# A chunked RWKV-7 recurrence with its first product in one full-width matmul, under a list schedule of best-of-six passes

## The chip, the cores and the metric

The kernel runs on one core of a Trainium2 chip. The metric is device microseconds (us) of one execution, smaller is better. The engines are named as the profile names them: PE multiplies matrices (PEld loads its weights), DVE and ACT work on vectors, POOL does slower vector work, SP issues DMAs.

## The reference

One layer of a hybrid decoder trunk, sequence 4096, width 1024, float32. The input is normalised, projected by one matrix of 3728 columns, and read by two groups of heads: four heads of gated linear attention (GLA), and eight RWKV-7 heads of size 64. Their outputs are gated, concatenated, projected, added to the input and normalised. The part that this change is about is the RWKV-7 state update, one step per token:

```python
def step(S, inp):
    r_t, w_t, k_t, v_t, kk_t, a_t = inp
    sa = jnp.einsum('bhvk,bhk->bhv', S, -kk_t)
    S = (S * w_t[:, :, None, :]
         + sa[..., None] * (kk_t * a_t)[:, :, None, :]
         + v_t[..., None] * k_t[:, :, None, :])
    y = jnp.einsum('bhvk,bhk->bhv', S, r_t)
    return S, y
```

Every head has a 64x64 state. Each token decays it, corrects it along one direction (the delta rule), adds an outer product, and reads it with `r_t`.

## The kernel before, in words

**Tiling.** The sequence is cut into 8 blocks of 512 tokens (`TB`). Eight heads are handled as four pairs `p`, one head on partitions 0 to 63 (`lo`) and one on 64 to 127 (`hi`). A *unit* `u` is one pair in one block, so there are 32 units. Inside a unit the tokens are taken in `NC` = 8 chunks of 64 (`C`). All projections are float16 matmuls in a high part and a low part, three products of 8 matmuls of 512 columns each (`proj`, L732). Everything in the recurrence is float32, and the profile shows each float32 matmul as two weight loads and two matmul passes.

**A unit.** `rwkv_ab` (L779) makes the operands of a unit and works out the coefficients between tokens of one chunk. The products of 64 keys with 128 columns land in PSUM as `pe` and `po`, and masked copies (`copy_predicated`) put them into three tiles: `De` and `Do` (one per head, 128 columns per chunk) and `Nb` (192 columns per chunk). The diagonal 32x32 blocks of `Nb` go through DRAM to POOL, which inverts them by substitution (`Tc`, `tm`), and back. `rwkv_i` (L910) completes the inverse. Projections write the value rows to a tile `v`; the scaled keys are transposed into `bk`, and the value rows into the odd halves of `sv`, a tile of 8 chunks x 2 heads x 64 columns whose other half holds the state.

**The recurrence** is `rwkv_c` (L934). Chunk by chunk:

1. two matmuls with 128 rows and 64 columns of weights, one per head, give the residual in bank `ch`; ACT copies it to `us` (one copy on 128 partitions);
2. two more matmuls of that form add the output of the chunk to the bank `y`, which is held through the whole unit;
3. ACT scales the state with the decay `PC` into `psd` (two instructions on 64 partitions);
4. one 128x128 matmul multiplies `us` by the inverse in `Nb`; ACT copies the result into `sv`, over the state (two copies on 64 partitions);
5. one 128x128 matmul with 128 columns gives the update of the state, and DVE adds it to `psd`, two instructions, into the `sv` of the next chunk.

After the last chunk 16 matmuls of 64x64 add the rest of the output to `y`, and ACT copies `y` out to `cy`.

**Order of the work.** The kernel is written as generators that run beside one another (streams for the recurrence, for the units' operands, GLA, projections, the output). They are not run in the order of the text. `Engine` (L326) records every operation as a `Step` with a duration from `cost` (L311), a delay until others see its result (`lag`), and its dependencies by half tile (`parts`, L102); `Array` (L125) models PE, with an extra 0.09 us when the shape of the occupied part of the array changes. `run` (L387) walks the streams once and gives a first start time to each step. Then `forward` (L233) is a list scheduler: on each engine that becomes free it takes, among the steps that can start, the one with the most urgent rank; `backward` (L283) turns the ends into latest starts, which are the next ranks. Two forward passes are made (L1386, L1387), the last one gives the order in which the instructions are issued, engine by engine. All engines work their queue in that order, so an instruction whose input is late holds up those behind it. In the profile every record has the line of the helper that issues them (L367), and one goes by tile names.

**PSUM.** Of the 8 banks, `ch` and `y` have one each and six (`NBK`, L45) go round among all streams through `need` and `rel`.

Of the kernel before, what the change touches and what calls it, by code (L numbers as in the profile page):

```python
# [20 lines left out]
P = 128  # L21
DM = 1024
KT = 8
TB = 512
# [19 lines left out]
PB = {"ch": 1, "y": 1}  # L44
NBK = 6  # L45
# [34 lines left out]
def hymba_kernel(ctx, tc, xT, wt, wg, wo, wua, gup, pk, ck, out):  # L80
# [16 lines left out]
    TABLES = ("pkt", "scl", "invs", "hinv", "mu_s", "omu_s", "carry", "wosc", "woinv", "gnh")  # L97
    now = [0.0]
# [3 lines left out]
    def parts(ap):  # L102
        if ap.tensor.name == out.tensor.name or ap.tensor.name.rsplit("_", 1)[0] in TABLES:
            return []
        if ap.space == DRAM:
            return [(ap.tensor.name, 0)]
        a = ap.start_partition()
        return [(ap.tensor.name, h) for h in range(a // 64, (a + ap.shape[0] - 1) // 64 + 1)]
# [16 lines left out]
    class Array:  # L125


        def __init__(self):
            self.tile, self.form, self.f32, self.free, self.clock = {}, None, False, 0.0, [0, 0.0, True]

        def put(self, t, d, cols, tiles):
# [11 lines left out]
            if full and f32 == 2 and not self.f32:  # L143
                d += 0.055
            for k in q:
                self.tile[k] = t + (d if full or not f32 else 0.66 * d)
            self.form, self.f32 = form, f32 > 0
# [85 lines left out]
    def forward(rank):  # L233
# [14 lines left out]
        for _ in steps:  # L248
# [11 lines left out]
            else:  # L260
                x = heapq.heappop(can[e])
            s = steps[x[1]]
# [63 lines left out]
    class Engine:  # L326
# [5 lines left out]
        def __getattr__(self, op):  # L332
            f = getattr(self.eng, op)

            def call(*a, **kw):
# [3 lines left out]
                if aps:  # L339
# [10 lines left out]
                    elif self.name == "D":  # L350
                        b = math.prod(o.shape) * (2 if o.dtype == F16 else 4)
                        d, lag = max(0.01, b / 3.6e5), 1.6 if ins[0].space == DRAM else 0.6
# [125 lines left out]
    De = [sb(un, [P, NC, P], F32, f"De{i}") for i in range(NBUF)]  # L478
    Do = [sb(un, [P, NC, P], F32, f"Do{i}") for i in range(NBUF)]
    Nb = [sb(un, [P, NC, 192], F32, f"Nb{i}") for i in range(NBUF)]  # L480
    SC = [sb(un, [P, 4, P], F32, f"SC{i}") for i in range(2)]
    for i in range(NBUF):
        G.memset(De[i], 0.0)
        V.memset(Do[i], 0.0)
        G.memset(Nb[i], 0.0)
# [201 lines left out]
    def x_block(b):  # L687
# [3 lines left out]
        for k in range(KT):  # L691
            xr = sb(rt, [P, TB], F32, *(("xr", NXR) if b > 0 else (("rk", "rn", "E", "ta", "kf", "r", "v", "cy")[k],)))
# [60 lines left out]
    def lora(WA):  # L753
# [5 lines left out]
        junk = sb(rt, [P, TB], F32, "E")  # L759
# [19 lines left out]
    def rwkv_ab(u, p, b, xs, LR):  # L779
        de, do, nb = De[u % NBUF], Do[u % NBUF], Nb[u % NBUF]  # L780
# [42 lines left out]
        for q_, d_ in ((lo, de), (hi, do)):  # L823
            V.tensor_tensor(d_[q_, :, 64:128], f3(r)[q_], EP[q_, :, 1:C + 1], ALU.mult)
# [3 lines left out]
        for q_, d_ in ((lo, de), (hi, do)):  # L828
            V.tensor_tensor(d_[q_, :, 0:64], f3(rn)[q_], EP[q_, :, 0:C], ALU.mult)
        for q_, ob, ok in ((lo, lo, hi), (hi, hi, lo)):  # L830
            V.scalar_tensor_tensor(bk[q_, :, ob], f3(ta)[q_], -0.5, EM[q_], ALU.mult, ALU.mult)
        yield after(bk, de, do)

        for c0 in range(0, NC, 4):
            pe, po = yield from need("r", 2)
            pe, po = f4(pe), f4(po)
            for i in range(4):
                T.matmul(pe[:, i, :], lhsT=bk[0:64, c0 + i, :], rhs=de[0:64, c0 + i, :], start=True, stop=True)
                T.matmul(po[:, i, :], lhsT=bk[64:128, c0 + i, :], rhs=do[64:128, c0 + i, :], start=True, stop=True)
            cc = slice(c0, c0 + 4)  # L840
            for q_, a_, ps in ((lo, slice(0, 3, 2), pe), (hi, slice(1, 3), po)):
                V.copy_predicated(nb[q_, cc].rearrange("p c (a t) -> p c a t", a=3)[:, :, a_],
                                  mc[q_].rearrange("p c (a t) -> p c a t", a=2), ps[q_].rearrange("p c (a t) -> p c a t", a=2))
            V.copy_predicated(de[64:128, cc, :], mc[64:128], pe[64:128])
            V.copy_predicated(do[0:64, cc, :], mc[0:64], po[0:64])
# [27 lines left out]
        v = shift((yield from proj((yield from get_w(W_RV + p, "r")), xs, "r")), 8 + p, tA("v"))  # L873
# [33 lines left out]
        units[u] = (de, do, nb, sv, bk, PC, bv, tg)  # L907
# [26 lines left out]
    def rwkv_c(p, b, mgt, st_):  # L934
        de, do, nb, sv, bkt, PC, bv, tg = st_
        yield after(nb, bkt, sv, ("y", 1))

        py = pbank("y").rearrange("p (c t) -> p c t", c=NC)
        st = Sst[p]
        S.copy(sv[0:64, 0, 0, :], st[0:64])  # L940
        V.tensor_copy(sv[64:128, 0, 1, :], st[64:128])
        dd = ((lo, de, 0), (hi, do, 1))
        for c in range(NC):
            pc = pbank("ch").rearrange("p (a t) -> p a t", a=8)
            for q_, d_, e in dd:
                T.matmul(pc[q_, 0, :], lhsT=d_[:, c, 0:64], rhs=sv[:, c, e, :], start=True, stop=True)
            us = sb(rt, [P, 64], F32, "us", 2)
            S.copy(us, pc[:, 0, :])
            for q_, d_, e in dd:
                T.matmul(py[q_, c, :], lhsT=sv[:, c, e, :], rhs=d_[:, c, 64:128], start=c == 0, stop=False)  # L950
            psd = sb(rt, [P, 64], F32, "psd", 2)
            for q_, d_, e in dd:
                S.activation(psd[q_], sv[q_, c, e, :], AF.Copy, scale=PC[q_, c])
            yield after(us) + XL
            T.matmul(pc[:, 1, :], lhsT=nb[:, c, 0:P], rhs=us, start=True, stop=True)
            S.copy(sv[lo, c, 0, :], pc[lo, 1, :])
            S.copy(sv[hi, c, 1, :], pc[hi, 1, :])
            yield after(sv) + XL
            T.matmul(pc[:, 2:4, :], lhsT=bkt[:, c, :], rhs=sv[:, c], start=True, stop=True)
            for q_, d_, e in dd:  # L960
                dst = sv[q_, c + 1, e, :] if c < NC - 1 else st[q_]
                V.scalar_tensor_tensor(dst, pc[q_, 2 + e, :], PC[q_, c], psd[q_], ALU.mult, ALU.add)
            if c < NC - 1:
                yield after(sv, ("ch", 1)) + XL
        for c in range(NC):
            for q_, d_, e in dd:
# [486 lines left out]
```

## Time and profile before

| What | Value |
|---|---|
| Time, median of 3 runs (lowest to highest) | 2420.46 us (2418.77 to 2423.89) |
| Span of the profiled execution, first to last instruction | 2418.4 us |
| The profiled execution's own time | not listed apart; the median lies 2.1 us above its span |
| Busy: PE, DVE, ACT, POOL | 95%, 71%, 50%, 35% of the span |
| Mean granted clock of PE | 0.981 |
| Moved by DMA | 325.54 MB, mean 135 GB/s |

A busy share counts the time in which an engine had an instruction under way. PE's matmuls are pipelined: a 512-column matmul is shown as 0.38 us long while the next one may start 0.22 us after it, so the time that one costs is read from start to start, not from its length. In the tables of waits, the engine named first stood idle until the one behind the arrow had finished.

### The profile page before, as it was taken

To read this page: it belongs to the slowest core of one execution; us is meant where nothing else is said; L and a number is where in the kernel's file an instruction comes from. 1 tells how busy PE (TensorE), PEld (TensorE's weight loads), DVE (VectorE), ACT (ScalarE), POOL (GpSimd) and SP (SyncE) were. 2 spreads that over 40 slices of the span, in tenths; PEclk is the share of its full clock that TensorE was granted. 3 is DMA by queue.
4 is the path that set the end of the run, shared out by engine and by line. 5 is a ranking of instruction groups with operands and counts; after the bars stand their busy time and mean duration, and the time that the engine had idled before them with its cause. 6 is when DMAs were issued, how large, how long until landed. Compare 5 with 4: busy or idle time off the path is not lost. (4 is left out here: it accounts for less than half of the span.)

```text
span 2418.4 us, 54463 instructions
## 1 busy us (share of the span) xinstructions
PE 2288.9 (95%) x20710; PEld 1341.4 (55%) x20710; DVE 1705.4 (71%) x3866; ACT 1218.6 (50%) x3123; POOL 856.8 (35%) x2217
## 2 busy tenths in 40 slices
PE   7898999999999999999999999999999998999986
PEld 3555565555565556556564565655565564655653
DVE  7777968568775776677676677666867577666766
ACT  7566575454544554454644545445445455444442
POOL 3441233424434442325334143353433353232400
PEclk8998999999999999999999999999999999999988
DMA  6666545455334543446424553345533454344432
GB/s 187 208 208 190 163 147 169 120 171 154 91 103 120 172 130 90 121 121 191 119 84 122 162 151 104 104 118 169 155 91 104 122 170 129 99 112 115 141 83 74
DMA packets 275387, 325.54 MB, mean 135 GB/s; under 512 B 131652, under 2 KB 132788, under 8 KB 275124
## 3 DMA queue, kind: packets, MB, share of 16 engines
q1 hardware_dynamic: 275124, 322.06, 45.8%
q8 instruction: 162, 2.65, 0.5%
q14 instruction: 101, 0.83, 0.1%
HBM read 276.90 MB, written 45.05 MB: 133 GB/s over the span
## 5 line engine op out<-in xcount | busy, mean ns | idle before, releaser
L367 PE MATMUL bank<-x,wr 128*128 128x512 f16 x3264 | 806.5, 381 | 14.5 <-ACT x L367 3.9
L367 POOL TENSOR_TENSOR tm<-Tc,f 128x60 f32<-128x60 f32 (+24 forms) x961 | 341.6, 356 | 675.8 <-DMA f<-nd 531.4
L367 PEld LDWEIGHTS <-wr 128*128 128x128 f16 x3264 | 309.2, 100 | 320.8 <-issue 29.3
L367 PE MATMUL bank<-x,wg 128*128 128x512 f16 x1536 | 391.4, 382 | 4.4 <-DVE rgs L367 1.8
L367 POOL TENSOR_TENSOR Tc<-Tc,tm 128x60 f32<-128x60 f32 (+24 forms) x961 | 345.4, 359 | 73.7
L367 PE MATMUL bank<-x,wo 128*128 128x512 f16 x1488 | 363.2, 381 | 0.2
L367 DVE SCALAR_TENSOR_TENSOR sv<-ch,PC,psd 64x64 f32<-64x64 f32 x448 | 126.2, 282 | 210.4 <-PE ch L367 201.9
L367 POOL TENSOR_TENSOR xacc<-xacc,xr 128x512 f32<-128x512 f32 x98 | 130.8, 1334 | 390.4 <-ACT xr L367 204.5
L367 ACT ACTIVATE psd<-sv,PC 64x64 f32<-64x64 f32 x512 | 171.9, 342 | 138.9 <-DVE sv L367 131.9
L367 PEld LDWEIGHTS <-wg 128*128 128x128 f16 x1536 | 145.5, 100 | 149.4 <-issue 12.2
L367 PEld LDWEIGHTS <-wo 128*128 128x128 f16 x1488 | 141.5, 101 | 135.9 <-issue 6.0
L367 PEld LDWEIGHTS <-x 128*128 128x128 f16 x3120 | 190.7, 100 | 32.8 <-issue 13.4
L367 PE MATMUL bank<-wg,x 128*128 128x128 f16 x3072 | 206.6, 221 | 2.2 <-DMA wg<-wdr 2.2
L367 ACT COPY sv<-ch 64x64 f32<-64x64 f32 x512 | 104.8, 205 | 100.6 <-PE ch L367 94.0
L367 ACT ACTIVATE sa<-bank,mu_s 128x512 f32<-128x512 f32 x104 | 71.4, 687 | 144.1 <-PE bank L367 143.2
L367 PEld LDWEIGHTS ch<-us,Nb 128*128 128x128 f32 x512 | 87.3, 191 | 63.2 <-ACT us L367 47.9
L367 POOL MEMSET Tc<- 32x8 f32 (+1 forms) x160 | 23.9, 149 | 272.2 <-DMA td<-Tc 227.4
L367 PEld LDWEIGHTS ch<-sv,bk 128*128 128x128 f32 x512 | 90.4, 190 | 50.3 <-ACT sv L367 34.8
L367 PE MATMUL ch<-sv,bk 128*128 128x128 f32 x512 | 104.9, 287 | 10.2 <-ACT sv L367 10.0
L367 ACT COPY us<-ch 128x64 f32<-128x64 f32 x256 | 53.4, 209 | 112.9 <-PE ch L367 111.1
L367 PE MATMUL ch<-us,Nb 128*128 128x64 f32 x512 | 95.8, 269 | 11.9 <-ACT us L367 10.5
L367 PEld LDWEIGHTS ch<-sv,De 128*64 128x64 f32 x512 | 49.3, 135 | 95.6 <-issue 41.7
(327 smaller groups left out, 4109.2 us busy)
## 6 DMA issues: line engine op xcount, KB each, us to landing
wr<-wdr SPq DMA_DIRECT2D x256, 256.0 KB
wg<-wdr SPq DMA_DIRECT2D x184, 256.0 KB
xr<-in_xT_dram SPq DMA_DIRECT2D x176, 256.0 KB
wo<-wdr SPq DMA_DIRECT2D x128, 256.0 KB
f<-nd SPq DMA_DIRECT2D x128, 128.0 KB
x<-in_wt_dram SPq DMA_DIRECT2D x29, 512.0 KB
wdr<-wo SPq DMA_DIRECT2D x25, 512.0 KB
out_dram<-mgg SPq DMA_DIRECT2D x33, 256.0 KB
```

Source lines behind the costliest of these rows:

```text
L367: put(t0, self.name, d, lag, cols, tiles, tab, outs, ins, lambda: f(*a, **kw))
```

## The change

The arithmetic of the recurrence is regrouped, and the scheduler is changed.

*The recurrence.* `De`, `Do` and `Nb` become one tile `W` of seven 64-column blocks per chunk (448 columns, two buffers): blocks 0 and 1 hold the coefficients of the residual for the two heads, block 2 the decayed `r`, 3 and 4 the matrix that is inverted, 5 and 6 the coefficients of the output. The residual is one 128x128 matmul with 128 columns, of whose result each head uses one quarter, so ACT copies `us` in two instructions on 64 partitions. The state of each chunk is also copied into a new tile `Ss` (two ACT copies per chunk, from chunk 1 on, and one per unit at its start), `psd` is made from `Ss` by one instruction on 128 partitions, and it is issued after the copies into `sv`. The output matmuls leave the loop: after the last chunk come 16 matmuls of 64x64 from `Ss` and 16 with 128 rows and 64 columns from `sv`. Bank `y` is no longer held through the unit; the output takes one of the shared banks at the end, and there are seven of those. The decayed `r` is written by one DVE instruction on 128 partitions where there were two on 64. The tile `v` is given up: the value rows and the low-rank input take `E`, and two scratch uses go to `rn` and `crs`.

*The scheduler.* The tiles `W` and `sv` are tracked in blocks of 64 columns; the model of PE charges weight loads of full float32 matmuls; a transfer that reads DRAM lands after 2.0 us (2.7 for a broadcast) where it was 1.6. In `forward`, when DVE or ACT would take a step, it looks at the four earliest of those that cannot start yet: if one of them can start within 0.7 of the step's duration and is more urgent by more than the wait, the engine waits for it. After the first pass six passes are made, and the one with the lowest end by the model's own count is issued.

```diff
@@ -41,8 +41,8 @@
-PB = {"ch": 1, "y": 1}
-NBK = 6
+PB = {"ch": 1}
+NBK = 7
@@ -95,6 +95,7 @@
+    FINE = ("W0_", "W1_", "sv_")
@@ -105,7 +106,16 @@
-        return [(ap.tensor.name, h) for h in range(a // 64, (a + ap.shape[0] - 1) // 64 + 1)]
+        halves = range(a // 64, (a + ap.shape[0] - 1) // 64 + 1)
+        if ap.tensor.name.rsplit("_", 1)[0][:-1] not in FINE:
+            return [(ap.tensor.name, h) for h in halves]
+        row, *dims = ap.ap
+        cols = {ap.offset % row[0]}
+        for st_, n in dims[:-1]:
+            cols = {x + st_ * i for x in cols for i in range(n)}
+        w = dims[-1][0] * (dims[-1][1] - 1)
+        blocks = {y for x in cols for y in range(x // 64, (x + w) // 64 + 1)}
+        return [(ap.tensor.name, h, y) for h in halves for y in blocks]
@@ -126,7 +136,7 @@
-            self.tile, self.form, self.f32, self.free, self.clock = {}, None, False, 0.0, [0, 0.0, True]
+            self.tile, self.form, self.f32, self.one, self.free, self.clock = {}, None, False, 0.0, 0.0, [0, 0.0, True]
@@ -140,11 +150,12 @@
-            if full and f32 == 2 and not self.f32:
-                d += 0.055
+            if full and f32 == 2:
+                load = 0.107 * (c[1] - c[0]) / 4
+                d = max(0.0, load - self.one) + max(d / 2, load) + d / 2
-            self.form, self.f32 = form, f32 > 0
+            self.form, self.f32, self.one = form, f32 > 0, d / max(f32, 1)
@@ -230,7 +241,7 @@
-    def forward(rank):
+    def forward(rank, ahead=0.0):
@@ -259,6 +270,14 @@
+                if e in "VS":
+                    soon = [w for w in heapq.nsmallest(4, wait[e]) if w[0] < t + ahead * steps[x[1]].d and rank[w[1]] < x[0] - (w[0] - t)]
+                    if soon:
+                        w = min(soon, key=lambda w: rank[w[1]])
+                        heapq.heappush(can[e], x)
+                        wait[e].remove(w)
+                        heapq.heapify(wait[e])
+                        x = (rank[w[1]], w[1])
@@ -349,7 +368,9 @@
-                        d, lag = max(0.01, b / 3.6e5), 1.6 if ins[0].space == DRAM else 0.6
+                        d, lag = max(0.01, b / 3.6e5), 0.6
+                        if ins[0].space == DRAM:
+                            lag = 2.0 + 0.7 * (o.space != DRAM and ins[0].ap[0][0] == 0)
@@ -475,14 +496,12 @@
-    De = [sb(un, [P, NC, P], F32, f"De{i}") for i in range(NBUF)]
-    Do = [sb(un, [P, NC, P], F32, f"Do{i}") for i in range(NBUF)]
-    Nb = [sb(un, [P, NC, 192], F32, f"Nb{i}") for i in range(NBUF)]
+    Wt = [sb(un, [P, NC, 448], F32, f"W{i}") for i in range(NBUF)]
+    Ss = sb(un, [P, NC, 64], F32, "Ss")
-        G.memset(De[i], 0.0)
-        V.memset(Do[i], 0.0)
-        G.memset(Nb[i], 0.0)
+        for c in range(NC):
+            (G if c % 2 else V).memset(Wt[i][:, c], 0.0)
...
@@ -756,7 +775,7 @@
-        junk = sb(rt, [P, TB], F32, "E")
+        junk = sb(rt, [P, TB], F32, "rn")
@@ -777,7 +796,8 @@
-        de, do, nb = De[u % NBUF], Do[u % NBUF], Nb[u % NBUF]
+        W = Wt[u % NBUF].rearrange("p c (a t) -> p c a t", a=7)
+        nb = Wt[u % NBUF][:, :, 192:320]
@@ -820,29 +840,28 @@
         hot.append(u)
-        for q_, d_ in ((lo, de), (hi, do)):
-            V.tensor_tensor(d_[q_, :, 64:128], f3(r)[q_], EP[q_, :, 1:C + 1], ALU.mult)
+        V.tensor_tensor(W[:, :, 2, :], f3(r), EP[:, :, 1:C + 1], ALU.mult)
         for q_, ob, ok in ((lo, lo, hi), (hi, hi, lo)):
         V.scalar_tensor_tensor(r, r, pkt[:, PK_RK + p:PK_RK + p + 1], kf, ALU.mult, ALU.mult)
-        for q_, d_ in ((lo, de), (hi, do)):
-            V.tensor_tensor(d_[q_, :, 0:64], f3(rn)[q_], EP[q_, :, 0:C], ALU.mult)
+        for e, q_ in enumerate((lo, hi)):
+            V.tensor_tensor(W[q_, :, e, :], f3(rn)[q_], EP[q_, :, 0:C], ALU.mult)
         for q_, ob, ok in ((lo, lo, hi), (hi, hi, lo)):
             V.scalar_tensor_tensor(bk[q_, :, ob], f3(ta)[q_], -0.5, EM[q_], ALU.mult, ALU.mult)
-        yield after(bk, de, do)
+        yield after(bk, Wt[u % NBUF][:, :, 0:192])
 
             for i in range(4):
-                T.matmul(pe[:, i, :], lhsT=bk[0:64, c0 + i, :], rhs=de[0:64, c0 + i, :], start=True, stop=True)
-                T.matmul(po[:, i, :], lhsT=bk[64:128, c0 + i, :], rhs=do[64:128, c0 + i, :], start=True, stop=True)
+                for e, (q_, ps) in enumerate(((lo, pe), (hi, po))):
+                    T.matmul(ps[:, i, :].rearrange("p (a t) -> p a t", a=2), lhsT=bk[q_, c0 + i, :], rhs=W[q_, c0 + i, e:3:2 - e, :],
+                             start=True, stop=True)
             cc = slice(c0, c0 + 4)
-            for q_, a_, ps in ((lo, slice(0, 3, 2), pe), (hi, slice(1, 3), po)):
-                V.copy_predicated(nb[q_, cc].rearrange("p c (a t) -> p c a t", a=3)[:, :, a_],
-                                  mc[q_].rearrange("p c (a t) -> p c a t", a=2), ps[q_].rearrange("p c (a t) -> p c a t", a=2))
-            V.copy_predicated(de[64:128, cc, :], mc[64:128], pe[64:128])
-            V.copy_predicated(do[0:64, cc, :], mc[0:64], po[0:64])
+            for e, (qb, qk, ps) in enumerate(((lo, hi, pe), (hi, lo, po))):
+                for q_, a_ in ((qb, slice(3 + e, 6 + e, 2)), (qk, slice(e, 6 + e, 5))):
+                    V.copy_predicated(W[q_, cc, a_, :], mc[q_].rearrange("p c (a t) -> p c a t", a=2),
+                                      ps[q_].rearrange("p c (a t) -> p c a t", a=2))
         rel("r")
@@ -870,7 +889,7 @@
-        v = shift((yield from proj((yield from get_w(W_RV + p, "r")), xs, "r")), 8 + p, tA("v"))
+        v = shift((yield from proj((yield from get_w(W_RV + p, "r")), xs, "r")), 8 + p, tA("E"))
...
@@ -932,43 +951,48 @@
     def rwkv_c(p, b, mgt, st_):
-        de, do, nb, sv, bkt, PC, bv, tg = st_
-        yield after(nb, bkt, sv, ("y", 1))
-        py = pbank("y").rearrange("p (c t) -> p c t", c=NC)
+        W, nb, sv, bkt, PC, bv, tg = st_
+        yield after(nb, bkt, sv)
         st = Sst[p]
-        S.copy(sv[0:64, 0, 0, :], st[0:64])
-        V.tensor_copy(sv[64:128, 0, 1, :], st[64:128])
-        dd = ((lo, de, 0), (hi, do, 1))
+        S.copy(sv[lo, 0, 0, :], st[lo])
+        V.tensor_copy(sv[hi, 0, 1, :], st[hi])
+        S.copy(Ss[:, 0, :], st)
+        dd = ((lo, 0), (hi, 1))
         for c in range(NC):
             pc = pbank("ch").rearrange("p (a t) -> p a t", a=8)
-            for q_, d_, e in dd:
-                T.matmul(pc[q_, 0, :], lhsT=d_[:, c, 0:64], rhs=sv[:, c, e, :], start=True, stop=True)
+            T.matmul(pc[:, 0:2, :], lhsT=W[:, c, 0:2, :].rearrange("p a t -> p (a t)"), rhs=sv[:, c], start=True, stop=True)
             us = sb(rt, [P, 64], F32, "us", 2)
-            S.copy(us, pc[:, 0, :])
-            for q_, d_, e in dd:
-                T.matmul(py[q_, c, :], lhsT=sv[:, c, e, :], rhs=d_[:, c, 64:128], start=c == 0, stop=False)
+            for q_, e in dd:
+                S.copy(us[q_], pc[q_, e, :])
+            if c > 0:
+                for q_, e in dd:
+                    S.copy(Ss[q_, c, :], sv[q_, c, e, :])
             psd = sb(rt, [P, 64], F32, "psd", 2)
-            for q_, d_, e in dd:
-                S.activation(psd[q_], sv[q_, c, e, :], AF.Copy, scale=PC[q_, c])
             yield after(us) + XL
-            T.matmul(pc[:, 1, :], lhsT=nb[:, c, 0:P], rhs=us, start=True, stop=True)
-            S.copy(sv[lo, c, 0, :], pc[lo, 1, :])
-            S.copy(sv[hi, c, 1, :], pc[hi, 1, :])
+            T.matmul(pc[:, 2, :], lhsT=nb[:, c, :], rhs=us, start=True, stop=True)
+            for q_, e in dd:
+                S.copy(sv[q_, c, e, :], pc[q_, 2, :])
+            S.activation(psd, Ss[:, c, :], AF.Copy, scale=PC[:, c])
             yield after(sv) + XL
-            T.matmul(pc[:, 2:4, :], lhsT=bkt[:, c, :], rhs=sv[:, c], start=True, stop=True)
-            for q_, d_, e in dd:
+            T.matmul(pc[:, 4:6, :], lhsT=bkt[:, c, :], rhs=sv[:, c], start=True, stop=True)
+            for q_, e in dd:
                 dst = sv[q_, c + 1, e, :] if c < NC - 1 else st[q_]
-                V.scalar_tensor_tensor(dst, pc[q_, 2 + e, :], PC[q_, c], psd[q_], ALU.mult, ALU.add)
+                V.scalar_tensor_tensor(dst, pc[q_, 4 + e, :], PC[q_, c], psd[q_], ALU.mult, ALU.add)
             if c < NC - 1:
                 yield after(sv, ("ch", 1)) + XL
+        py = (yield from need("y")).rearrange("p (c t) -> p c t", c=NC)
         for c in range(NC):
-            for q_, d_, e in dd:
-                T.matmul(py[q_, c, :], lhsT=sv[q_, c, e, :], rhs=nb[q_, c, P:192], start=False, stop=c == NC - 1)
+            for q_, e in dd:
+                T.matmul(py[q_, c, :], lhsT=Ss[q_, c, :], rhs=W[q_, c, 2, :], start=c == 0, stop=False)
+        for c in range(NC):
+            for q_, e in dd:
+                T.matmul(py[q_, c, :], lhsT=sv[:, c, e, :], rhs=W[:, c, 5 + e, :], start=False, stop=c == NC - 1)
         yield lambda: done["C"] == done["CC"]
         S.copy(y, py.rearrange("p c t -> p (c t)"))
+        rel("y")
         S.activation(rs, y, AF.Square)
...
@@ -1333,7 +1357,7 @@
-            WA = shift((yield from proj((yield from get_w(W_WA, "r")), xs, "r")), 12, sb(rt, [P, TB], F32, "v"))
+            WA = shift((yield from proj((yield from get_w(W_WA, "r")), xs, "r")), 12, sb(rt, [P, TB], F32, "E"))
...
@@ -1384,7 +1408,12 @@
-        start, end = forward(backward(end))
+        best = None
+        for _ in range(6):
+            start, end = forward(backward(end), 0.7)
+            if best is None or max(end) < best[0]:
+                best = max(end), start
+        start = best[1]
```

More of the change, by code (lines that the diff above doesn't have):

```diff
@@ L691, in x_block @@
         for k in range(KT):
-            xr = sb(rt, [P, TB], F32, *(("xr", NXR) if b > 0 else (("rk", "rn", "E", "ta", "kf", "r", "v", "cy")[k],)))
+            xr = sb(rt, [P, TB], F32, *(("xr", NXR) if b > 0 else (("rk", "rn", "E", "ta", "kf", "r", "crs", "cy")[k],)))
             if b > 0:
@@ L906, in rwkv_ab @@
         S.copy(sv[0:64, :, 1, :], pv[0:64])
-        units[u] = (de, do, nb, sv, bk, PC, bv, tg)
+        units[u] = (W, nb, sv, bk, PC, bv, tg)
         done["A"] += 1
@@ L1240, in out_last @@
                 if i == 1:
-                    sq.append(sb(rt, [P, TB], F32, ("rk", "rn", "E", "ta", "kf", "r", "v", "cy")[n]))
+                    sq.append(sb(rt, [P, TB], F32, ("rk", "rn", "E", "ta", "kf", "r", "crs", "cy")[n]))
                     S.activation(sq[n], part[n], AF.Square)
@@ L1345, in stream_i @@
             yield lambda: done["A"] > u
-            yield from rwkv_i(units[u][2])
+            yield from rwkv_i(units[u][1])
             done["I"] += 1
```

## Prediction

> **What bounds the kernel now.** I read the page first, for the busy shares and the granted clock.
>
> ```profile
> span 2418.4 us, 54463 instructions
> PE 2288.9 (95%) x20710; PEld 1341.4 (55%) x20710; DVE 1705.4 (71%) x3866; ACT 1218.6 (50%) x3123; POOL 856.8 (35%) x2217
> PEclk8998999999999999999999999999999999999988
> ```
>
> PE is busy for 95% of the span, and outside the ends it is granted its full clock. DVE and ACT have room. Then the table by stages (time, and busy time of PE, PEld, DVE, ACT, POOL), to see where PE is not full.
>
> ```profile
> 0.00:200.00 200.00, 163.44 (x1230) 93.12 (x1230) 152.88 (x424) 129.16 (x254) 83.58 (x183) 0.92 0.67 203
> 200.00:2300.00 2100.00, 2034.12 (x18684) 1196.55 (x18685) 1480.54 (x3243) 1047.86 (x2750) 773.25 (x2034) 0.99 0.45 131
> 2300.00:2418.00 118.00, 91.32 (x797) 51.68 (x795) 71.94 (x201) 41.62 (x120) 0.00 (x0) 0.85 0.27 79
> ```
>
> In the long middle PE lacks 2100 - 2034.12 = 66 us, at the start 37 us and at the end 27 us. So the middle is PE's, and what an edit is worth there is read from PE, start to start. The timeline of PE round one chunk shows the price of each step (start, length, matmuls):
>
> ```profile
> 1199.19 0.81 PE L367 MATMUL bank<-x,wg 128*128 128x512 f16 x3
> 1199.93 0.27 PE L367 MATMUL ch<-sv,De 128*64 128x64 f32 x1
> 1199.94 0.27 PE L367 MATMUL ch<-sv,Do 128*64 128x64 f32 x1
> 1200.04 0.22 PE L367 MATMUL ch<-sv,De 128*64 128x64 f32 x1
> ...
> 1200.10 0.22 PE L367 MATMUL y<-De,sv 128*64 128x64 f32 x1
> ...
> 1200.16 0.22 PE L367 MATMUL y<-Do,sv 128*64 128x64 f32 x1
> 1200.32 0.39 PE L367 MATMUL bank<-x,wg 128*128 128x512 f16 x1
> 1200.55 0.38 PE L367 MATMUL bank<-x,wr 128*128 128x512 f16 x1
> 1200.76 0.33 PE L367 MATMUL ch<-us,Nb 128*128 128x64 f32 x2
> 1200.93 1.46 PE L367 MATMUL bank<-x,wg 128*128 128x512 f16 x6
> 1202.22 0.38 PE L367 MATMUL ch<-sv,bk 128*128 128x128 f32 x2
> 1202.44 0.59 PE L367 MATMUL bank<-x,wg 128*128 128x512 f16 x2
> ```
>
> Six float16 matmuls take 1.46 us with the last one 0.38 long, so (1.46 - 0.38)/5 = 0.216 us from start to start. The third of the first row starts at 1199.62, its follower is due at 1199.84. The group of four small products (residual and output, two passes each) begins at 1199.93, 0.09 us late, and the stream goes on at 1200.32: the group costs 0.48 us, though its passes, side by side for the two heads, follow one another at 0.06 us once they run (1200.04, 1200.10, 1200.16), 0.24 for the four pairs. The other 0.24 us lie in the change of shape, ahead and behind. The product with the inverse costs 1200.93 - 1200.55 - 0.216 = 0.16 us, and the full 128x128 one with 128 columns 1202.44 - 1200.93 - 6 x 0.216 = 0.21 us: neither changes the shape, and the stream runs on beside them. At the end of a unit:
>
> ```profile
> 1966.51 0.38 PE L367 MATMUL bank<-x,wr 128*128 128x512 f16 x1
> 1966.82 1.15 PE L367 MATMUL y<-Nb,sv 64*64 64x64 f32 x32
> 1967.90 0.39 PE L367 MATMUL bank<-x,wr 128*128 128x512 f16 x1
> ```
>
> The 16 output products cost 1967.90 - 1966.51 - 0.216 = 1.17 us. A unit thus takes 8 x (0.48 + 0.16 + 0.21) + 1.17 = 7.97 us of PE in the recurrence, 255 us in 32 units.
>
> **The change, part by part.**
>
> *PE.* The residual becomes one product of exactly the form of the last step of a chunk, so I price it by that row: 0.21 us, with no change of shape. A chunk then costs 0.21 + 0.16 + 0.21 = 0.58 us where it was 0.85. The output, now after the loop, has 16 products of 64x64 (the form of the row above, 1.17 us) and 16 of 128 rows by 64 columns, which the trace of before shows only inside the group. Its lower bound is 16 pairs of passes at 0.06 = 0.96 us, the upper one the 1.17 us of the other form with its own change of shape. I take 1.17, since the two batches have different shapes. A unit: 8 x 0.58 + 2.34 = 6.98 us, 0.99 less (1.20 with the lower bound). In the last unit PE isn't full, so I count 31 units: -31 us, bounds -31 and -37.
>
> A rule speaks against this: the Trainium skill, "TensorEngine Tiling (Array Packing)", under "When to Use Tiling" and "Theoretical Speedup", puts weights of up to 64 columns into column tiles, for up to twice the speed, and this edit takes such tiles apart and throws half of the product away. In passes the trace agrees (0.12 us for the two heads against 0.21), and by passes alone, 8 x 0.09 + 0.96 us more on 31 units, the change would cost some 52 us. The measured group, with its change of shape inside, is why my sum has the other sign.
>
> *ACT.* The groups of ACT and of the two DVE instructions that are merged:
>
> ```profile
> L367 ACT ACTIVATE psd<-sv,PC 64x64 f32<-64x64 f32 x512 | 171.9, 342 | 138.9 <-DVE sv L367 131.9
> L367 ACT COPY sv<-ch 64x64 f32<-64x64 f32 x512 | 104.8, 205 | 100.6 <-PE ch L367 94.0 <-PE y L367 0.7
> L367 ACT COPY us<-ch 128x64 f32<-128x64 f32 x256 | 53.4, 209 | 112.9 <-PE ch L367 111.1
> L367 ACT COPY sv<-Sst 64x64 f32<-64x64 f32 x32 | 7.7, 240 | 0.2
> L367 DVE TENSOR_TENSOR Do<-r,EP 64x512 f32<-64x512 f32 x32 | 24.4, 762 | 0.8
> L367 DVE TENSOR_TENSOR De<-r,EP 64x512 f32<-64x512 f32 x32 | 23.0, 717 | 8.6 <-PE y L367 8.3
> ```
>
> The second copy of `us` adds 256 x (2 x 0.205 - 0.209) = 51 us; `Ss` takes 480 copies at the 0.240 us of the copy from the state, 115 us; `psd` loses half of its instructions, -86 us. ACT goes up by 80 us, to 54% of the span. That is hidden in 1200 us of idle ACT, except for 0.205 us per chunk on the path: the second `us` copy lies between the residual and the product with the inverse. In exchange only two copies of 0.24, and no longer two `psd` of 0.342, can stand ahead of the copies into `sv`.
>
> *DVE.* One merged instruction per unit at about 0.76 us replaces 0.762 + 0.717: -23 us on an engine with 700 us idle: 0. It waits for the output of the unit two before, which now ends later (8.3 us of wait today); with 2.34 us of output in place of 1.17 some 7 waits would be a microsecond longer, and DVE isn't the bound: 0.
>
> *`v` in `E`.* The decay of the next unit cannot be written before the bonus of this one has read the values. In two of the 31 places the order of before has it the other way; the first:
>
> ```profile
> 721.24 0.78 ACT L367 ACTIVATE E<-bank,half_p,usc 128x512 f32<-128x512 f32 x1
> 730.92 0.80 DVE L367 TENSOR_TENSOR bv<-bv,v 128x512 f32<-128x512 f32 x1
> ```
>
> There the operands of a unit would be 10.5 us later. The recurrence of a unit runs beside a full PE, with the next unit's operands made ahead, so I take 0, at most 2 x 10.5 = 21 us.
>
> *The schedule.* What a better order can win is read from the table of waits (total, times, longest):
>
> ```profile
> PEld ch L367 <- ACT us L367: 47.9, 146, 2.0
> DVE bv L367 <- DMA bv<-bcdb: 44.0, 19, 6.9
> PEld ch L367 <- ACT sv L367: 34.8, 118, 1.7
> PEld ch L367 <- DVE sv L367: 26.5, 40, 1.7
> DVE rn L367 <- DMA rn<-bcda: 21.5, 19, 3.0
> ```
>
> In 47.9 + 34.8 + 26.5 = 109 us PE's weight loads stood for the recurrence: its matmul was queued before its input came, and all projections behind it stood too. Part of that is DVE itself standing for a broadcast that landed later than planned (44.0 and 21.5 us), with the state updates queued behind; landing times of 2.0 and 2.7 us in the plan move those instructions back. Waiting for the more urgent step and taking the best of six passes aim at the same 109 us. The gain lies between nothing and all of it; an order that is best by the model's count need not be best on the chip, so I take a quarter, -27 us. Against it stands the second `us` copy, which lengthens a wait only where PE waits already or comes to: between 0 and 256 x 0.205 = 52 us; with a quarter of the 146 places, +7 us. The bank that `y` gives up is included here. Holding DVE or ACT idle up to 0.7 of a step costs them time that they have.
>
> *The tail.* The end of the last unit stands on the chain:
>
> ```profile
> 2380.12 1.08 PE y L367 x32
> ```
>
> It becomes twice as many passes, +1.1 us if none of them are done before the loop's end, and eight second copies add up to 1.6 us, while PE's savings there are worth little. I take +2 us.
>
> **Sum.** -31 - 27 + 7 + 2 = -49 us on the span of 2418.4, so 2369. The execution's own time isn't listed; the median of the runs lies 2.1 us above the span, and I carry that over: 2371 us.
>
> **The rivals.**
>
> *The second copy shows on PE (slower).* If the order puts the product with the inverse right where the first copy alone would have let it start, every chunk holds PE for 0.205 us more: +52 us, with no gain from the order and the +2 of the tail: 2420.5 - 31 + 54 = 2443. Without a gain from the order it is slower once over 29/0.205 = 141 of the 256 chunks show the copy. For it: PE waits for ACT there in 146 places already. Against it: the planner has a price for that copy, and other work to put in.
>
> *The change of shape stays.* If the full-width residual still drained the array, at 0.48 us, nothing would be saved in the loop and the outputs would come on top: 31 x 1.17 = +36 us, 2457. The row of the same form at 0.21 us speaks against it. This is the case nearest to the rule above.
>
> *No difference.* If the saved PE time turns into waits, because what sets the pace is the delay from one step of the recurrence to the next, the time stays at 2420. The 66 us that PE lacks in 2100 speak against it.
>
> *The order wins far more.* Two thirds of the 109 us and the lower output bound: 2420.5 - 37 - 73 + 9 = 2320, and halfway to the forecast 2345. For it: six tries against one, and a model nearer to the chip.
>
> **How the numbers follow.** Forecast (about 2350 to 2412) 0.62; the larger gain, below 2350, 0.16; no difference 0.07; the second copy 0.12; the shape 0.03. A measurement of this kernel can tell about 0.2%, 4.8 us, from no change, so faster is 0.62 + 0.16 = 0.78, same 0.07, slower 0.15. The range takes the forecast, "no difference", and the nearer parts of the two neighbours: from 2330 (a third of the larger gain, 0.05, left out) to 2428 (0.11 to 0.12 of the slower cases left out).
>
> **What would show it.** In the changed profile: the residual in one group of 128x128 with 128 columns, 512 records, costing 0.21 us from start to start; `y` only after the loops, two batches of 32 passes, about 1.2 us each or less; PE's busy time some 30 us lower; ACT up by about 80 us; the sum of PE's waits for `us` and `sv` below 109 us. I am wrong if the residual costs clearly over 0.25 us, if PE's idle time in the middle grows by more than 30 us, or if PE's busy time does not fall.

## The result, and the profile after

The changed kernel takes 2330.69 us (median of 4 runs, 2325.62 to 2331.08). The kernel before took 2422.18 us on the same chip. The ratio is 0.9621, with a 95% interval from 0.9601 to 0.9641: 3.8% less time, about 92 us. The forecast was 2371 us, 49 us less. The kernel before was timed again beside each group of experiments and had medians between 2416.6 and 2423.9 us, so I compare ratios, each to the kernel before as timed beside it, with its interval.

The same views of the kernel after, first the page:

```profile
span 2323.8 us, 53920 instructions
PE 2237.5 (96%) x20198; PEld 1373.7 (59%) x20198; DVE 1704.6 (73%) x3840; ACT 1309.4 (56%) x3603; POOL 854.9 (37%) x2221
PEclk9999999999999999999999999999999999999999
```

PE is still what is full. Its busy time fell by 51 us and its idle time by 43, from 129.5 to 86.3 us. The 2000 us in the middle, in both kernels, first before, then after (time, busy time of PE, PEld, DVE, ACT, POOL, the granted clock):

```profile
200.00:2200.00 2000.00, 1937.27 (x17812) 1139.85 (x17813) 1401.78 (x3073) 1005.27 (x2639) 743.37 (x1965) 0.99 0.46 131
```

```profile
200.00:2200.00 2000.00, 1972.56 (x18094) 1217.94 (x18093) 1462.70 (x3163) 1118.44 (x3168) 774.30 (x2034) 1.00 0.46 135
```

PE stands for 27 us there instead of 63. The price of each step, in PE's timeline after (start, length, matmuls):

```profile
1170.38 1.04 PE L388 MATMUL bank<-x,wr 128*128 128x512 f16 x4
1171.25 0.38 PE L388 MATMUL ch<-sv,W 128*128 128x128 f32 x2
1171.47 1.46 PE L388 MATMUL bank<-x,wr 128*128 128x512 f16 x6
1172.77 0.33 PE L388 MATMUL ch<-us,W 128*128 128x64 f32 x2
1172.93 1.46 PE L388 MATMUL bank<-x,wr 128*128 128x512 f16 x6
1174.23 0.38 PE L388 MATMUL ch<-sv,bk 128*128 128x128 f32 x2
1174.45 0.81 PE L388 MATMUL bank<-x,wr 128*128 128x512 f16 x3
...
1284.66 1.03 PE L388 MATMUL bank<-x,wr 128*128 128x512 f16 x4
1285.62 1.15 PE L388 MATMUL bank<-W,Ss 64*64 64x64 f32 x32
1286.70 1.15 PE L388 MATMUL bank<-W,sv 128*64 128x64 f32 x32
1287.78 1.47 PE L388 MATMUL bank<-x,wo 128*128 128x512 f16 x6
```

The residual now goes by without a gap ahead of it: 1171.25 is where the next float16 matmul would have begun. It costs 1171.47 - 1170.38 - 4 x 0.216 = 0.23 us, the product with the inverse 0.16, the last one 0.22. The two batches of output cost 1287.78 - 1284.66 - 4 x 0.216 = 2.26 us. A unit: 8 x 0.61 + 2.26 = 7.14 us, where the prediction had 6.98 and the kernel before 7.97. This chunk is no exception: where such a step stands between two 512-column float16 matmuls, the median over the whole trace is 0.22 us for the residual (173 of the 256 chunks), and 0.48 us for the group of four small products of before (143 of 256). And the waits (total, times, longest):

```profile
DVE bv L388 <- DMA bv<-bcdb: 8.2, 6, 2.9
PEld ch L388 <- ACT sv L388: 21.3, 53, 1.4
PEld ch L388 <- DVE sv L388: 15.2, 37, 1.3
PEld ch L388 <- ACT us L388: 13.0, 28, 2.1
DVE rn L388 <- DMA rn<-bcda: 6.0, 6, 2.3
```

PE's waits for the recurrence are 21.3 + 15.2 + 13.0 = 49.5 us, against 109. DVE's two waits for broadcasts, which were 44.0 and 21.5 us, are 8.2 and 6.0.

One more row of this table fell: the time in which weight loads into `ch` stood and waited for nothing that the profile shows ("issue"). Here it is before, in schedule_only (an experiment below: the old recurrence under the new scheduler), and after:

```profile
PEld ch L367 <- issue: 48.5, 129, 2.7
```

```profile
PEld ch L388 <- issue: 43.0, 121, 0.4
```

```profile
PEld ch L388 <- issue: 7.1, 29, 0.4
```

It goes with the form of the recurrence and not with the scheduler. I read it as a part of what the changes of shape cost; the profile itself does not name the cause.

### The profile page after: what moved, and what is told of

It is laid out like the page before. It is cut to its first block, busy times and chain, and to the rows that moved or that the text cites. A ratio compares the mean times of both kernels' runs of the same rounds, so it can differ in the third digit from the quotient of the medians.

```text
span 2323.8 us, 53920 instructions
## 1 busy us (share of the span) xinstructions
PE 2237.5 (96%) x20198; PEld 1373.7 (59%) x20198; DVE 1704.6 (73%) x3840; ACT 1309.4 (56%) x3603; POOL 854.9 (37%) x2221
## 4 chain that ended last, share of the span: by engine, by line
PE 75%; DVE 14%; ACT 5%; DMA 3%; issue 2%; POOL 1%; SPq 0%; DVEq 0%; ACTq 0%
PE bank L388 68%; PE ch L388 7%; DVE W L388 2%; DMA wdr<-wo 2%; DVE nta L388 2%; DVE mgg L388 1%; DVE bk L388 1%; DVE mgr L388 1%; ACT gep L388 1%; DVE gbc L388 1%; DVE E L388 1%; DVE sv L388 1%; ACT L388 1%; ACT wo L388 1%; DVE kf L388 0%
## 5 line engine op out<-in xcount | busy, mean ns | idle before, releaser
L388 PE MATMUL bank<-x,wr 128*128 128x512 f16 x3264 | 823.4, 381 | 9.2 <-ACT x L388 3.5
L388 PEld LDWEIGHTS <-wr 128*128 128x128 f16 x3264 | 315.2, 100 | 302.0 <-issue 25.0
L388 PE MATMUL bank<-x,wg 128*128 128x512 f16 x1536 | 398.8, 379 | 0.0
L388 PE MATMUL bank<-x,wo 128*128 128x512 f16 x1488 | 357.3, 380 | 0.0
L388 PE MATMUL bank<-wg,x 128*128 128x128 f16 x3072 | 201.0, 220 | 1.4 <-DVE rgs L388 1.1
L388 DVE COPY_PREDICATED W<-mc,bank 64x512 f32<-64x512 uint8 x256 | 180.2, 724 | 9.6 <-PE bank L388 5.0
L388 ACT COPY us<-ch 64x64 f32<-64x64 f32 x512 | 104.9, 205 | 126.4 <-PE ch L388 120.4
L388 ACT COPY Ss<-sv 64x64 f32<-64x64 f32 x448 | 107.8, 241 | 114.2 <-DVE sv L388 101.4
L388 PEld LDWEIGHTS ch<-sv,bk 128*128 128x128 f32 x512 | 90.3, 190 | 47.4 <-ACT sv L388 21.3
L388 PEld LDWEIGHTS ch<-sv,W 128*128 128x128 f32 x512 | 91.2, 191 | 41.7 <-DVE sv L388 15.2
L388 PEld LDWEIGHTS ch<-us,W 128*128 128x128 f32 x512 | 90.4, 190 | 41.2 <-ACT us L388 13.0
```

Of the source, the lines that this page charges most:

```text
L388: put(t0, self.name, d, lag, cols, tiles, tab, outs, ins, lambda: f(*a, **kw))
```

## The experiments

The first question is how the gain divides between the regrouped recurrence and the scheduler, the second which part of the scheduler carries it.

### recurrence_only: the new recurrence under the scheduler of before

Against the kernel after:

```diff
-        halves = range(a // 64, (a + ap.shape[0] - 1) // 64 + 1)
...
-        return [(ap.tensor.name, h, y) for h in halves for y in blocks]
+        return [(ap.tensor.name, h) for h in range(a // 64, (a + ap.shape[0] - 1) // 64 + 1)]
...
-        for _ in range(6):
-            start, end = forward(backward(end), 0.7)
+        start, end = forward(backward(end))
```

PE's model and the landing times are those of before, too.

> The regrouped recurrence under the scheduler of before (half-tile tracking, the old model of PE, landing after 1.6 us, no waiting for a more urgent step, one pass). Theory (PE's work and the order of the work add up): the changes of shape that go save 31 us of PE, the rest of the gain stays with the scheduler, so about 2390 us. Rival 1 (the new form of the recurrence also takes PE's waits away): about 2345. Rival 2 (the form gains only under a scheduler that knows its costs): 2410 or above.

Measured: 2429.68 us, ratio 1.0061 [1.0044, 1.0077]. It is 0.6% slower than before, although its instructions are those of the kernel after. In this order they cost more: PE is busy for 2309.4 us, 72 more than in the kernel after. Some 19 us of that would fit the lower clock (0.984 against 0.992). The timeline of this kernel round the 64x128 products of one unit shows one place where more of it goes, PE first, then DVE:

```profile
1215.76 1.16 PE L368 MATMUL bank<-W,bk 64*128 64x128 f32 x16
...
1219.53 0.81 PE L368 MATMUL bank<-x,wr 128*128 128x512 f16 x3
1220.27 1.16 PE L368 MATMUL bank<-W,bk 64*128 64x128 f32 x16
1221.36 0.39 PE L368 MATMUL bank<-x,wr 128*128 128x512 f16 x1
```

```profile
1217.20 3.00 DVE L368 COPY_PREDICATED W<-mc,bank 64x512 f32<-64x512 uint8 x4
```

The second half of the products starts at 1220.27, just after the four masked copies of the first half have ended (1217.20 + 3.00). Nothing in the data asks for that: these copies write other columns of `W` than the products read. A planner that tracks half tiles cannot see it, since `W` is one tile where there were three. Over the whole trace I count 98 separate groups of these products, against 45 before and 40 after, and each group pays its changes of shape: this half costs 1221.36 - 1219.53 - 3 x 0.216 = 1.18 us, two halves 2.36, where a whole group costs 2.08 (the median in recurrence_fine, the next run). The theory missed by 40 us and rival 1 by more. Rival 2 has the number, "2410 or above"; the next run shows how much of it is the tracking.

### recurrence_fine: the same, with fine tracking

Against recurrence_only:

```diff
-        return [(ap.tensor.name, h) for h in range(a // 64, (a + ap.shape[0] - 1) // 64 + 1)]
+        halves = range(a // 64, (a + ap.shape[0] - 1) // 64 + 1)
...
+        return [(ap.tensor.name, h, y) for h in halves for y in blocks]
```

> The regrouped recurrence under the scheduler of before, but with W and sv tracked in 64-column blocks. Theory (half-tile tracking is wrong for the merged tile W: the planner sees clashes in it that are none, and cuts the 64x128 products of a unit in parts; with fine tracking the saved changes of shape come through): 2416.6 - 31, about 2386 us, with the 64x128 products in fewer, longer groups again. Rival (the form needs the waiting for a more urgent step, since its chunk has more ACT steps): 2410 or above.

Measured: 2414.03 us, ratio 0.9965 [0.9939, 0.9990]. The groups are 44 again, so the cut products are mended, and that brings 1.0%, 23 us, against recurrence_only. The cuts themselves account for about 54 x 0.28 = 15 us of it, an estimate from the prices above. But only 0.35% (0.10 to 0.61) comes through of the 1.3% (31 us) that the PE work promises. The rival has the time; its reason, the chunk's extra ACT steps, does not show, since PE's three waits for `us` and `sv` are 28.6 + 30.4 + 34.6 = 93.6 us, less than the 109 of before. PE is busy for 2278.8 us of a span of 2414.7, 10 us less than before, and stands idle for 136 us, 6 us more.

### lookahead_only: the kernel before, DVE and ACT waiting for a more urgent step

```diff
-        start, end = forward(backward(end))
+        start, end = forward(backward(end), 0.7)
```

with the added lines of `forward`, and nothing else.

> The kernel before; the only edit is that DVE and ACT wait for a more urgent step, in the one pass that there was. Theory A (the waiting carries most of the scheduler's 60 us): about 2375 us, with PE's waits for us and sv clearly below 109 us. Theory B (it works only with six passes or with the later landing): above 2400.

Measured: 2388.53 us, ratio 0.9846 [0.9819, 0.9873]: 1.5% in one edit of the order. The time lies between theory A (2375) and theory B (above 2400), and what theory A was to be known by, a clear fall of the waits, did not come. The waits of this kernel:

```profile
PEld ch L375 <- ACT us L375: 52.6, 160, 2.2
PEld ch L375 <- ACT sv L375: 33.1, 113, 2.6
PEld ch L375 <- DVE sv L375: 18.8, 31, 1.6
```

They add up to 104.5 us, hardly less than the 109 of before. What fell is PE's idle time as a whole, from 129.5 to 2389.8 - 2276.5 = 113.3 us, and its busy time, by 12 us with the same instructions. The profile also shows a higher mean clock. The rows of the cores (span, mean granted clock), before, this kernel, after:

```profile
core 0: 2418.4 us, clock 0.981
```

```profile
core 0: 2389.8 us, clock 0.987
```

```profile
core 0: 2323.8 us, clock 0.992
```

What is missing to the full clock is 0.019 x 2418 = 46 us, then 31, and 19 in the kernel after. The 15 us between the first two are about the 12 us of busy time, but that the order won them is not shown. Of the 46 us, 0.08 x 200 + 0.15 x 118 = 34 lie at the two ends (the prediction's table by stages), where PE isn't full. Executions of one kernel differ too: the kernel before, timed beside this one, had clocks from 0.981 to 0.987, and the one at 0.987 took 2426.26 us, more than their median of 2423.93. recurrence_only had 0.984 to 0.991 and is slower than before. Which waits of PE became shorter here stays open.

### recurrence_fine_waiting: both together

The kernel of recurrence_fine with the edit of lookahead_only:

```diff
-        start, end = forward(backward(end))
+        start, end = forward(backward(end), 0.7)
```

> The regrouped recurrence, fine tracking, and DVE and ACT waiting for a more urgent step; landing times, PE's model and the one pass are those of before. Theory A (the form needs an order that starts the chunk's steps on time, and the waiting gives it): the waiting on the recurrence of before gave 35 us and the form saves 31 us of PE, together 2420 - 66, about 2355 us. Theory B (the form keeps only the 10 us that it showed without the waiting): about 2375 us.

Measured: 2354.23 us, ratio 0.9742 [0.9720, 0.9763]. Theory A gave this time. Under this order the new form, with the fine tracking and the bank that come with it, is worth 1.0% against lookahead_only, 25 us; under the greedy order (one that never leaves an engine waiting) it was worth 0.35%. PE is busy for 2250.1 us, 26 less than in lookahead_only, and its three waits fell to 65.3 us from the 93.6 of recurrence_fine, as theory A's reason would have it.

### schedule_only: the old recurrence under the whole new scheduler

```diff
+    FINE = ("De0_", "De1_", "Do0_", "Do1_", "Nb0_", "Nb1_", "sv_")
```

and the scheduler's functions of after; `De`, `Do`, `Nb` and the held bank `y` stay.

> The recurrence of before under the whole new scheduler, its tiles De, Do, Nb and sv tracked in 64-column blocks, bank y still held. Theory: 60 us less, the fall of PE's waits for us and sv, so about 2360 us, with those waits near 50 us. Rival 1 (the form does most of it): 2400 or above, with waits near 109 us.

Measured: 2357.1 us, ratio 0.9749 [0.9730, 0.9768]. The time is as forecast, 60 us less, and the waits are only part of the way:

```profile
PEld ch L388 <- ACT us L388: 32.9, 133, 1.2
PEld ch L388 <- ACT sv L388: 24.3, 120, 0.8
PEld ch L388 <- DVE sv L388: 22.3, 44, 1.9
```

79.5 us, where theory said near 50. The page of this kernel gives PE's busy time:

```profile
span 2347.4 us, 54489 instructions
PE 2266.5 (97%) x20710; PEld 1337.5 (57%) x20710; DVE 1717.1 (73%) x3866; ACT 1231.5 (52%) x3123; POOL 851.5 (36%) x2217
```

Against before, PE is idle for 49 us less (80.9, from 129.5) and busy for 22 us less. With the new form on top, 0.9749 becomes 0.9621: 1.3%, 31 us. Between these two kernels PE's busy time falls by 29.0 us, from 2266.5 to 2237.5, and its idle time grows by 5. The 31 us hold all that the recurrence brings, the seventh bank and the second copy of `us` included; the fall of the busy time is the measure nearest to the PE work alone.

### The parts of the scheduler, each taken out of the kernel after

Four kernels leave out one part each, and a fifth makes one pass. coarse_parts undoes the edit of `parts` alone:

```diff
-        return [(ap.tensor.name, h, y) for h in halves for y in blocks]
+        return [(ap.tensor.name, h) for h in range(a // 64, (a + ap.shape[0] - 1) // 64 + 1)]
```

> The kernel after with half-tile tracking in the scheduler alone (the dependencies on the chip stay as they are). Theory A (fine tracking is what lets the order start chunks early): 20 us or more above the kernel after. Theory B (the planner's knowledge of DMA and of waiting does it): within 8 us of the kernel after.

no_lookahead:

```diff
-            start, end = forward(backward(end), 0.7)
+            start, end = forward(backward(end), 0.0)
```

> The kernel after without DVE and ACT waiting for a more urgent step, still best of six passes. Theory A (the waiting is what shortens PE's waits for us and sv): 15 us or more above the kernel after, those waits back towards 109 us. Theory B (it is a small part): within 8 us.

old_landing:

```diff
-                        d, lag = max(0.01, b / 3.6e5), 0.6
-                        if ins[0].space == DRAM:
-                            lag = 2.0 + 0.7 * (o.space != DRAM and ins[0].ap[0][0] == 0)
+                        d, lag = max(0.01, b / 3.6e5), 1.6 if ins[0].space == DRAM else 0.6
```

> The kernel after with reads of DRAM planned to land after 1.6 us, as before, broadcasts too. Theory A (DVE standing for broadcasts that come later than planned costs PE time): 8 us or more above 2331, with DVE's waits for broadcasts back towards 66 us for bv and rn. Theory B (that wait is hidden): within 6 us.

old_array undoes the edit of `Array`:

```diff
-            if full and f32 == 2:
-                load = 0.107 * (c[1] - c[0]) / 4
-                d = max(0.0, load - self.one) + max(d / 2, load) + d / 2
+            if full and f32 == 2 and not self.f32:
+                d += 0.055
```

> The kernel after with the planner's old price of full float32 products (0.055 us more for the first one after a float16 matmul, no weight load). Theory A (some 0.1 us per product is too little to change the order's worth): within 8 us of 2331. Theory B (the planner now sends the products of the recurrence too early, and PE's waits for us and sv rise from 50 us): 15 us or more above.

one_pass:

```diff
-        for _ in range(6):
+        for _ in range(1):
```

> The kernel after with one pass in place of the best of six. Theory A (the choice among six is a small part): within 10 us of 2331. Theory B (it is a main part): 20 us or more above.

| Kernel | Median, us | Ratio to before [95%] | Lost against 0.9621 |
|---|---|---|---|
| no_lookahead | 2375.90 | 0.9834 [0.9819, 0.9849] | 2.1% |
| coarse_parts | 2366.03 | 0.9794 [0.9779, 0.9808] | 1.7% |
| old_array | 2347.16 | 0.9721 [0.9694, 0.9748] | 1.0% |
| old_landing | 2356.07 | 0.9714 [0.9688, 0.9740] | 0.9% |
| one_pass | 2337.27 | 0.9638 [0.9612, 0.9664] | 0.2%, intervals overlap |

The waiting and the fine tracking matter most. In no_lookahead the three waits of PE add up to 30.9 + 29.7 + 20.3 = 80.9 us; theory A had the size, and part of the mechanism. In coarse_parts theory A's time came, and its reason, chunks that start late, does not show: these waits stay near those of after, 53.7 us, and PE's idle time too (85.4 us against 86.3), while there are 100 groups of 64x128 products instead of 40, the same cut as in recurrence_only, and PE is busy for 42 us more. For old_landing theory A's time came (8 us or more), but what it was to be known by did not: DVE's waits for `bv` and `rn` are 12.5 and 9.4 us, 8 more than after, and not back towards 66. For old_array theory B's time came and its mechanism did not: PE's three waits are 44.1 us, below those of after. How those two parts gain their 16 to 25 us stays open. The choice among six passes is a small part, as theory A had it: 4 us by the ratios, 7 by the medians, not clear of the noise. The four other parts lose 5.7% together where the whole change gained 3.8%. So the parts need one another: without one of them the others bring less, and each figure holds only beside the others.

### us_twice: two more copies on the path

```diff
                 S.copy(us[q_], pc[q_, e, :])
+                S.copy(us[q_], pc[q_, e, :])
```

> The kernel after with each of the two copies of us made twice over: two more ACT copies of 0.205 us per chunk on the path from the residual to the product with the inverse, 512 in all, 105 us of ACT, known to the planner. Theory (the order hides such copies; the second us copy of the change cost nearly nothing): at most 10 us above 2331. Rival (each one holds PE): 50 us or more above.

Measured: 2347.99 us, ratio 0.9718 [0.9698, 0.9738], 1.0% or 23 us above the kernel after by the ratios, 17 by the medians. Neither number came true, it lies between. 512 copies of 0.205 us are 105 us, of which 23 arrive: 0.045 us per copy. For the 256 second copies that the change itself added, that makes 12 us, an estimate from this run; by the medians it would be 8, and each edit also gives a new order.

### six_banks: no bank gained

```diff
-NBK = 7
+NBK = 6
```

> The kernel after with six shared PSUM banks, the eighth bank left unused, so that the streams have no more banks than before. Theory A (the bank given up by y is a small part): within 8 us of 2331. Theory B (PE waited for banks): 15 us or more above.

Measured: 2340.39 us, ratio 0.9679 [0.9654, 0.9705], 0.6% or 14 us above the kernel after by the ratios, 10 by the medians; the intervals do not touch. It lies between the two theories. A new set of banks also gives a new order, so I read it as a small part, and not as a price of a bank.

## Why the prediction was right, and where its sizes were off

The direction and the mechanism on PE held, point by point. That the time lies within the range is luck: 2330.69 us is 0.7 us above its lower end, and the forecast had about half of the gain.

*PE's work.* The residual without a change of shape was priced at 0.21 us and costs 0.22 to 0.23; the outputs were priced at 2.34 and cost 2.26. By these rows a unit saves 7.97 - 7.14 = 0.83 us, 26 us in 31 units, where the sum had 31. PE's busy time falls by 26 us (lookahead_only to recurrence_fine_waiting) and by 29 us (schedule_only to the kernel after). The whole fall of 51 us, where some 30 were forecast, is this and the scheduler's 22. The times of the same pairs differ by 25 and 31 us, but in them the bank (10 to 14 us by six_banks) and the second copy are counted too. The step that the prediction missed is its condition: the saving came through only under an order that knows the new tile and lets DVE and ACT wait for the more urgent step. Under the old scheduler the same PE work made the kernel 0.6% slower. The rival "no difference" named that way of losing it; the 66 us of PE's idle time that the prediction held against it did not exclude it.

*The order* is the term that was mis-sized. The prediction took "a quarter, -27 us" of the 109 us that PE's loads waited for the recurrence, and +7 us for the second copy, -20 together. The scheduler alone gives 60 us. The pot itself was the wrong one: lookahead_only gains 1.5% while these waits stay at 104.5 us, and schedule_only gains 60 us while they fall by 30. A wait that the table puts down to the recurrence was only part of what a better order could win. PE's idle time as a whole was the wider pot, 129.5 us, and it stood in the profile: schedule_only wins 49 us of it. Another 22 us came out of PE's busy time with the same instructions; the missing clock fell by about as much (from 0.019 to 0.010 of the span), but whether the order did that stays open. The bank that `y` gives up had no price of its own in the prediction; six_banks has 10 to 14 us there.

*The second copy of `us`* at +7 us: us_twice makes it 8 to 12, the right size as far as one run tells. The rival built on it (all 256 on PE, +52) did not come: twice as many cost 17 to 23. No run had the new form without the second copy.

*ACT* was to gain 80 us of work and gained 91; PE's waits for it fell all the same, from 47.9 + 34.8 to 13.0 + 21.3 us. *DVE*: the merged instruction takes 0.767 us, as priced, 24.5 us in all where the two took 24.4 + 23.0. DVE's busy time as a whole fell by 0.8 us and not by 23; why the rest of it grew stays open, and DVE isn't the bound.

```profile
L388 DVE TENSOR_TENSOR W<-r,EP 128x512 f32<-128x512 f32 x32 | 24.5, 767 | 1.9 <-PE bank L388 1.3
L388 ACT ACTIVATE E<-bank,half_p,usc 128x512 f32<-128x512 f32 x32 | 24.8, 776 | 8.7 <-PE bank L388 6.6 <-DVE pw L388 0.9 <-DVE bv L388 0.2
```

*`v` in `E`* cost nothing that this row shows: the decay stood 0.2 us for the bonus (`bv`), over all 32 units.

*The tail* was put at +2 us. From the end of the last copy of `y` (to `cy`) to the end of the span it is 42.3 us after and 36.5 before, 6 us more; schedule_only, with the old recurrence, has 43.3, and recurrence_fine_waiting 34.5. So this comes with the whole scheduler, and it lies behind the output products and cannot hold their cost. That cost is nearly hidden: in the last unit the first batch runs while the last chunk is still under way, and from the end of the last copies into `sv` to the end of the copy of `y` it is 2.2 us after and 2.1 before. What the second copies add to the tail was not measured.

*The shape rule.* The Trainium skill's rule for column tiles ("TensorEngine Tiling (Array Packing)", "When to Use Tiling") would, by passes alone, have made this change some 52 us slower, the prediction's estimate. In passes the trace agrees with it: 0.12 us for the two heads against 0.21. Beside a stream of full-width matmuls the 0.24 us of a change of shape is more than these 0.09 us that the tiles save.

The time came out between the two sums of the fourth rival, the larger gain from the order (2320 in full and 2345 halfway, given 0.16). Its cause is that rival's cause in kind: the order wins more. But that rival's reasons, six tries and two thirds of the 109 us, are not how it was won: one_pass loses little, and the waits fell by 60 us only with form and scheduler together.

## What to carry to other kernels

When PE is the bound, price a small matmul from start to start in the stream in which it stands: a shape that fits the data but not its neighbours can cost more than a wasteful one that lets the stream run on. An edit that merges tiles has to be told to whatever orders the work, or false clashes eat the gain. And do not bound what a better order can win by one row of waits: take the idle time of the bounding engine as a whole, and compare its busy time too, since another order of the same instructions gave PE up to 72 us more of it here.

## What the runs showed of the hardware

The price of a full float32 product of 128 columns was no surprise: 0.22 us in the float16 stream, before and after. A change of shape and back cost 0.24 us in that stream beyond the passes, and the order of the work decides how many there are: in recurrence_only 919 pairs of successive matmuls have different shapes, in the kernel after 742, with the same instructions. PE is busy for 72 us more there; the changes of shape are a part of that, and the rest stays open. What was missing to the full clock fell from 46 to 19 us between the profiled executions of the two kernels, with nearly the same matmuls. How much of that the order won, and how much time it was worth, no run here shows.
